# The gate product of the output weights moves from VectorE to GpSimd inside the attention phase

## The chip, the cores and the metric

The kernel runs on one core of a Trainium2 chip. The metric is the device time of one execution in microseconds, given as the median of several runs. The core's engines are TensorE (PE in the rows, its weight loads PEld), VectorE (DVE), ScalarE (ACT), GpSimd (POOL) and SyncE (SP, which issues transfers here). Each engine runs its own list of instructions in order, and waits on semaphores for the others.

## The reference, cut to what matters

One layer of a latent diffusion backbone: 2048 latent tokens and 256 context tokens of width 1024. A combined projection feeds a convolution group and an eight-head attention group; both are joined by one output projection, whose result is multiplied by the gate `g1` (one number per output column) and added to the residual:

```python
        conv_l = conformer_conv(u_l, conv_dw_w[i], conv_dw_b[i], conv_ln_g[i], conv_ln_b[i])
        y_l = merge_groups(conv_l, attn_l, w_o[i], b_o[i])
        x_mid = layer_norm(ALPHA * x + g1 * y_l, ln1_g[i], ln1_b[i])
```

`merge_groups` joins the two groups' outputs and multiplies them by `w_o`. A convolutional feed-forward part of the same layer follows. The kernel multiplies the gate into the columns of `w_o` beforehand, so that it is not applied to `y_l`.

## The kernel before, in words

**Precision.** Matrix products are made from pairs of values: a high part (a rounded copy) and a low part (the value minus its high part). `sub_lo` (L95) is the helper that makes a low part on the engine it is given, so many instructions bear line 95; they are told apart by tile. `mm3` makes the three matmuls of such a pair.

**Attention.** The loop over `u` runs through 128 query tiles of 128 rows: 8 heads (`h`) of 16 tiles (`qt`). Each iteration, in the written order:
- `scores(u)`: TensorE makes five chunks of scores (15 matmuls, L1044) into PSUM buffers `s`, VectorE takes the row maximum of each (L1046), of all (L1047) and scales it (L1048). The `s` buffers are seven; a tile uses five, and one more for turned values.
- `splits(u - 1)`: TensorE turns a part of the tile before (L1063), VectorE splits it into `pp` (L1068, L1069), and SyncE issues a transposing DMA of the rest, `pT<-ph` (L1080).
- `values`: TensorE's product with the values for the tile four earlier (L1094, L1095). Every fourth iteration `combine` does some small work on VectorE and GpSimd (L1115 to L1117).
- `exps(u)`: ScalarE's five exponentials (L1055) out of the `s` buffers, which they free; then a copy of the output (L1101).
- `his(u)`: ScalarE casts 1792 columns to `ph` (L1073), GpSimd makes their low part (L1074, the large subtraction).
- `k_split` when `qt` is 3 to 8: ScalarE casts (L824), GpSimd subtracts (tile `ktl`). `q_split` when `qt % 4 == 1`: ScalarE casts (L843), GpSimd subtracts (tile `ql`).
- `wo_split` when `u % 4 == 2` in iterations 78 to 106: the eight events of this document, numbered 1 to 8. It prepares one 128 x 512 piece of the output weights (four blocks of rows, two halves of columns).

The phase stands under a manual schedule for all engines: each engine gets its instructions in the order in which the code issues them.

**wo_split.** The piece `wst` is loaded on SyncE two iterations earlier (`wo_ld`, L1127), and the gate row `g1b`, repeated over all partitions, once before (L1183). Then: the product `wst * g1b` (L1139, in place), the cast to `woh` on ScalarE (L1140), and the low part `wol` on the engine given, which is GpSimd in the attention loop. In the code of an event the calls stand in this order:

```python
            his(ph, p32)
            ex[u] = ph, p32
            ...
            if WU <= u < WU + 32 and u % 4 == 2:
                wo_split((u - WU) // 8, (u - WU) // 4 % 2, wpa, G)
```

After the loop `wo_split` is called for blocks 4 to 7 as well; these take the other branch (L1137) with a further factor.

Of the kernel before, what the change touches and what calls it, by code (L numbers as in the profile page):

```python
# [15 lines left out]
ALU = mybir.AluOpType  # L16
# [63 lines left out]
def layer(ctx, tc, t, out):  # L80
    nc = tc.nc
    V, S, G, T = nc.vector, nc.scalar, nc.gpsimd, nc.tensor
# [11 lines left out]
    def sub_lo(eng, lo, full, hi):  # L94
        eng.tensor_tensor(lo, full, hi.bitcast(F32), op=ALU.subtract)  # L95
# [86 lines left out]
    def t2k(name):  # L182
        return p1.tile([P, 512], F32, tag="t2k", name=name, bufs=5)
# [71 lines left out]
    for ci, c0 in enumerate((0, D, 512)):  # L255
        ps = ptile("pada")
        for k in range(KB):
            w = t2k("wada")
# [9 lines left out]
            if k % 3 == 2:  # L268
                kd = ci * 2 + k // 3
                if kd < KB:  # L270
                    w = cvp.tile([P, 512], F32, tag="chn", name="wadad", bufs=3)
# [13 lines left out]
    for kd in range(6, KB):  # L285
        w = cvp.tile([P, 512], F32, tag="chn", name="wadad", bufs=3)
# [640 lines left out]
    for kind, g in stages:  # L927
        off, W = span(g)
        ntile = W // P
        if kind == "kv":  # L930
# [20 lines left out]
            for i in range(ntile):  # L951
                pv = ptile("pv")
                sl = slice(i * P, (i + 1) * P)
# [169 lines left out]
    g1b = wpa.tile([P, D], F32, name="g1b")  # L1123
# [6 lines left out]
    def wo_split(k, c, pl, eng):  # L1130
        w = wst.pop((k, c)) if k < 4 else wraw[k][:, c * 512:(c + 1) * 512]
        sl = slice(c * 512, (c + 1) * 512)
        if c == 0:
            woh[k] = pl.tile([P, D], F32R, name=f"woh{k}")
            wol[k] = pl.tile([P, D], F32R, name=f"wol{k}")
        if k >= 4:
            V.scalar_tensor_tensor(w, w, rv_c[:, k - 4:k - 3], g1b[:, sl], op0=ALU.mult, op1=ALU.mult)  # L1137
        else:
            V.tensor_tensor(w, w, g1b[:, sl], op=ALU.mult)  # L1139
        S.copy(woh[k][:, sl], w)  # L1140
        sub_lo(eng, wol[k][:, sl], w, woh[k][:, sl])

# [26 lines left out]
    for u in range(NU + LAG + 1):  # L1169
# [29 lines left out]
        w = u - LAG  # L1199
# [13 lines left out]
        if u < NU:  # L1213
            ph, p32 = exps(*st.pop(u))
            if w >= 0:
                evac(w, po)
            his(ph, p32)
            ex[u] = ph, p32
            if h + 1 < NH and 3 <= qt < 3 + KC:
                k_split(kstn, h + 1, slice(0, P) if h == 0 else k_half(h + 1, False), k_cols(qt - 3))  # L1220
            if qt % 4 == 1 and u + 4 < NU:
                qs_[u // 4 + 1] = q_split(ql_)
            if WU <= u < WU + 32 and u % 4 == 2:
                wo_split((u - WU) // 8, (u - WU) // 4 % 2, wpa, G)
            if u in (NU - 5, NU - 3, NU - 1):
                tt = (u - NU + 5) // 2
                if tt == 0:
                    e_hl = at1.tile([P, 2, 2, 4, P], F32R, tag="oh", name="e_hl", bufs=1)
                if tt < 2:
                    eh, el = e_hl[:, 0, tt], e_hl[:, 1, tt]  # L1230
                else:
                    e2 = k_tile().bitcast(F32R)[:, 0:1024].rearrange("p (s k n) -> p s k n", s=2, k=4)
                    eh, el = e2[:, 0], e2[:, 1]
                conv_split(early[tt], eh, el, G)
                early[tt] = (eh, el)
        elif w < NU:
            evac(w, po)
            wo_split(4 + u - NU, 0, wpb, V)
            wo_split(4 + u - NU, 1, wpb, G)
# [778 lines left out]
```

## Time and profile before

| what | value |
|---|---|
| median of 3 runs | 2864.55 us |
| lowest and highest | 2861.65 and 2869.92 us |
| the profiled execution's own time | 2868.03 us |
| its span, first to last instruction | 2866.3 us |
| TensorE busy | 2715.9 us, 95% |
| VectorE busy | 2257.8 us, 79% |
| ScalarE busy | 1699.1 us, 59% |
| GpSimd busy | 1605.1 us, 56% |
| chain that ended last | TensorE 64%, VectorE 13%, DMA 9%, ScalarE 6%, GpSimd 3% |

The rows further on come from one profiled execution. A row of a timeline gives the start, the duration, the engine, the line, the operation, the tile written and the tiles read, their shapes, how many alike are merged, and in brackets how long the engine stood idle before it and who released it. The shares of the table are means over phases with different bounds, so the phase of the change is read by itself.

### The profile page before, as it was taken

To read this page: it belongs to the slowest core of one execution; us is meant where nothing else is said; L and a number is where in the kernel's file an instruction comes from. 1 tells how busy PE (TensorE), PEld (TensorE's weight loads), DVE (VectorE), ACT (ScalarE), POOL (GpSimd) and SP (SyncE) were. 2 spreads that over 40 slices of the span, in tenths; PEclk is the share of its full clock that TensorE was granted. 3 is DMA by queue.
4 is the path that set the end of the run, shared out by engine and by line. 5 is a ranking of instruction groups with operands and counts; after the bars stand their busy time and mean duration, and the time that the engine had idled before them with its cause. 6 is when DMAs were issued, how large, how long until landed. Compare 5 with 4: busy or idle time off the path is not lost.

```text
span 2866.3 us, 46525 instructions
## 1 busy us (share of the span) xinstructions
PE 2715.9 (95%) x16222; PEld 2246.7 (78%) x16222; DVE 2257.8 (79%) x3918; ACT 1699.1 (59%) x3210; POOL 1605.1 (56%) x1131
## 2 busy tenths in 40 slices
PE   7999899899999999999898999999999999999988
PEld 4888787678888888887776888887778777888766
DVE  5767897888888899878857888887976888554787
ACT  3345456489989989876556555556555555433333
POOL 2235355578888898877435455546444443432555
PEclk8999999999999999999999999999999999999999
DMA  8742227599999999995388755657865788854665
GB/s 287 240 127 66 66 74 229 160 198 206 206 204 202 218 204 212 206 208 185 130 255 268 242 202 184 209 180 247 298 225 174 268 282 282 252 174 143 194 193 178
DMA packets 815483, 578.89 MB, mean 202 GB/s; under 512 B 505616, under 2 KB 654224, under 8 KB 814736
## 3 DMA queue, kind: packets, MB, share of 16 engines
q1 hardware_dynamic: 809136, 558.89, 71.6%
q10 hardware_dynamic: 6112, 17.04, 2.4%
q8 instruction: 127, 2.08, 0.3%
q14 instruction: 108, 0.88, 0.1%
HBM read 294.06 MB, written 164.31 MB: 160 GB/s over the span
## 4 chain that ended last, share of the span: by engine, by line
PE 64%; DVE 13%; DMA 9%; ACT 6%; issue 5%; POOL 3%; SPq 1%; ACTq 0%; DVEq 0%; POOLq 0%
PE px L1436 14%; PE s L1044 11%; PE prod L1436 10%; PE o L1094 4%; PE down L100 3%; PE down L98 3%; PE down L99 3%; DVE mx L1046 2%; PE o L1095 2%; PE tp L1063 1%; PE y L98 1%; PE y L99 1%; PE y L100 1%; DMA d_q<-qo 1%; DMA pT<-ph 1%
## 5 line engine op out<-in xcount | busy, mean ns | idle before, releaser
L1074 POOL TENSOR_TENSOR ph<-p,ph 128x1792 f16<-128x1792 f32 x128 | 463.2, 3619 | 98.2 <-ACT ph L1073 96.2
L1046 DVE TENSOR_REDUCE mx<-s 128x1 f32<-128x512 f32 (+1 forms) x640 | 389.4, 635 | 55.4 <-PE s L1044 52.8
L1055 ACT ACTIVATE p<-s,mx 128x512 f32<-128x512 f32 (+1 forms) x640 | 356.9, 649 | 72.6 <-DVE mx L1048 69.0
L95 POOL TENSOR_TENSOR wul<-s,wuh 128x512 fp32r<-128x512 f32 x176 | 243.9, 1391 | 238.0 <-ACT wuh L1427 224.3
L1436 PE MATMUL px<-oh,wuh 128*128 128x512 f32 x700 | 280.5, 401 | 19.0 <-ACT u L1770 9.9
L95 POOL TENSOR_TENSOR wul<-a,wuh 128x512 fp32r<-128x512 f32 x132 | 180.2, 1370 | 190.3 <-ACT wuh L1427 174.3
L1436 PE MATMUL px<-ol,wuh 128*128 128x512 f32 x700 | 277.5, 397 | 2.7 <-DVE ol L95 2.3
L1436 PE MATMUL px<-oh,wul 128*128 128x512 f32 x700 | 277.4, 396 | 0.0
L1044 PE MATMUL s<-kth,qh 128*128 128x512 f32 (+1 forms) x640 | 250.4, 391 | 13.2 <-ACT p L1055 7.7
L100 PE MATMUL down<-wdh,al 128*128 128x512 f32 x616 | 244.4, 397 | 8.9 <-DVE al L95 6.8
L98 PE MATMUL down<-wdh,ah 128*128 128x512 f32 x616 | 243.7, 396 | 7.4 <-ACT ah L1600 7.4
L99 PE MATMUL down<-wdl,ah 128*128 128x512 f32 x616 | 243.0, 394 | 0.0
L1044 PE MATMUL s<-kth,ql 128*128 128x512 f32 (+1 forms) x640 | 238.5, 373 | 0.2 <-POOL ql L95 0.2
L1044 PE MATMUL s<-ktl,qh 128*128 128x512 f32 (+1 forms) x640 | 237.8, 372 | 0.0
L1073 ACT CAST ph<-p 128x1792 f16<-128x1792 f32 x128 | 218.8, 1710 | 0.1
L1600 ACT CAST ah<-act 128x512 fp32r<-128x512 f32 x168 | 96.1, 583 | 188.6 <-PE down L99 138.1
L1436 PE MATMUL prod<-ol,wuh 128*128 128x512 f32 x524 | 206.4, 394 | 1.3 <-DVE ol L95 0.7
L1436 PE MATMUL prod<-oh,wuh 128*128 128x512 f32 x524 | 206.1, 393 | 0.4 <-ACT oh L1348 0.4
L1436 PE MATMUL prod<-oh,wul 128*128 128x512 f32 x524 | 205.9, 393 | 0.0
L1427 ACT CAST wuh<-s 128x512 fp32r<-128x512 f32 x176 | 108.6, 619 | 142.1 <-DVE s L1415 51.8
L1094 PE MATMUL o<-vh,pT 128*128 128x129 f16 x1792 | 173.0, 220 | 5.4 <-DMA pT<-ph 5.4
L1436 PEld LDWEIGHTS px<-oh,wuh 128*128 128x128 f32 x700 | 132.5, 189 | 57.5 <-ACT u L1770 15.1
(405 smaller groups left out, 7782.5 us busy)
## 6 DMA issues: line engine op xcount, KB each, us to landing
a<-in_w_up SPq DMA_DIRECT2D x154, 256.0 KB, 4.4
d_ws<-s SPq DMA_DIRECT2D x88, 256.0 KB, 2.3
s<-d_ws SPq DMA_DIRECT2D x88, 256.0 KB, 3.9
d_s<-sa SPq DMA_DIRECT2D x88, 256.0 KB, 3.2
d_t<-tw SPq DMA_DIRECT2D x77, 256.0 KB, 3.4
wd<-d_t SPq DMA_DIRECT2D x77, 256.0 KB, 3.9
sa<-d_act SPq DMA_DIRECT2D x66, 256.0 KB, 4.6
wada<-in_w_ada SPq DMA_DIRECT2D x16, 1024.0 KB, 5.7
```

The lines of the kernel that those rows point to most:

```text
L95: eng.tensor_tensor(lo, full, hi.bitcast(F32), op=ALU.subtract)
L98: T.matmul(ps, lhsT=lh, rhs=rh, start=first, stop=False)
L99: T.matmul(ps, lhsT=lh, rhs=rl, start=False, stop=False)
L100: T.matmul(ps, lhsT=ll, rhs=rh, start=False, stop=last)
L1044: T.matmul(ps[:, :w], lhsT=lq[:, qs], rhs=ks[:, c0:c0 + w], start=(n == 0), stop=(n == 2))
L1046: V.tensor_reduce(mx[:, a:a + 1], sl[a], axis=AX.X, op=ALU.max)
L1055: S.activation(p32[:, c0:c0 + w], sl[a], AF.Exp, scale=SCALE, bias=mx[:, NC_ + 1:NC_ + 2])
L1073: S.copy(ph[:, 0, :], p32[:, PT:])
L1074: G.tensor_tensor(ph[:, 1, :], p32[:, PT:], ph[:, 0, :], op=ALU.subtract)
L1094: T.matmul(po[:, 0:129], lhsT=hi, rhs=vh[:, kb, 0:129], start=(kb == 0), stop=False)
L1427: S.copy(h, w)
L1436: T.matmul(ps, lhsT=lw[:, k, :], rhs=rx[:, k, :], start=(fresh and k == 0 and n == 0), stop=(k == 3 and n == 2), skip_group_check=not fresh)
```

## The change

One line of `wo_split` is given to another engine: the product of a piece of the output weights with the gate row, in its branch for `k < 4`, is issued to GpSimd (`G`) in place of VectorE (`V`). The branch for `k >= 4` stays on VectorE.

```diff
@@ -1136,7 +1136,7 @@
         if k >= 4:
             V.scalar_tensor_tensor(w, w, rv_c[:, k - 4:k - 3], g1b[:, sl], op0=ALU.mult, op1=ALU.mult)
         else:
-            V.tensor_tensor(w, w, g1b[:, sl], op=ALU.mult)
+            G.tensor_tensor(w, w, g1b[:, sl], op=ALU.mult)
         S.copy(woh[k][:, sl], w)
         sub_lo(eng, wol[k][:, sl], w, woh[k][:, sl])
```

## Rows read from the trace of the kernel before

**Rows 1.** The head of the profile's page.

```profile
span 2866.3 us, 46525 instructions
```

**Rows 2.** Busy time by stretch: an ordinary part of attention, and the events' stretch.

```profile
core 0: us, PE busy (x) PEld busy (x) DVE busy (x) ACT busy (x) POOL busy (x), PEclk, DMA share, GB/s
700.00:800.00 100.00, 99.80 (x1056) 89.00 (x1054) 89.65 (x180) 93.29 (x149) 88.89 (x43) 1.00 1.12 206
990.00:1170.00 180.00, 170.23 (x1764) 149.00 (x1763) 168.21 (x306) 159.30 (x254) 159.94 (x77) 1.00 1.14 209
```

**Rows 3.** Timeline (start us, us, engine, line, operation), VectorE: tiles 48, 64, 76, 112.

```profile
840.31 0.16 DVE L1047 TENSOR_REDUCE mx<-mx 128x1 f32<-128x5 f32 x1
...
924.11 0.16 DVE L1047 TENSOR_REDUCE mx<-mx 128x1 f32<-128x5 f32 x1
...
988.53 0.16 DVE L1047 TENSOR_REDUCE mx<-mx 128x1 f32<-128x5 f32 x1
...
1188.78 0.16 DVE L1047 TENSOR_REDUCE mx<-mx 128x1 f32<-128x5 f32 x1
```

**Rows 4.** TensorE's waits, 990 to 1170 us: total us, times, longest us.

```profile
PE s L1044 <- ACT p L1055: 5.9, 6, 1.6
...
PE o L1094 <- DMA pT<-ph: 1.3, 2, 0.7
```

**Rows 5.** Instructions that touch tile wst: ns min/median/max, first and last start us.

```profile
L1139 DVE TENSOR_TENSOR wst<-wst,g1b x8: 2392/2414/4146, 1000.5 to 1157.7; 128x512 f32<-128x512 f32 x8
...
L95 POOL TENSOR_TENSOR wol<-wst,woh x8: 1260/1282/1297, 1007.6 to 1165.2; 128x512 fp32r<-128x512 f32 x8
```

**Rows 6.** The same view for lines 1137 and 1503, both after attention.

```profile
L1137 DVE SCALAR_TENSOR_TENSOR wraw<-wraw,rv_c,g1b x8: 726/742/1770, 1270.9 to 1291.2; 128x512 f32<-128x512 f32 x8
...
L1503 POOL TENSOR_TENSOR g1b<-g1b,bo x2: 1287/1508/1729, 1290.7 to 1293.4; 128x512 f32<-128x512 f32 x2
```

**Rows 7.** Timeline of VectorE, event 1.

```profile
1000.54 2.43 DVE L1139 TENSOR_TENSOR wst<-wst,g1b 128x512 f32<-128x512 f32 x1
```

**Rows 8.** Timeline of GpSimd, event 1 and the tile before.

```profile
998.79 3.63 POOL L1074 TENSOR_TENSOR ph<-p,ph 128x1792 f16<-128x1792 f32 x1 [1.59 <-ACT ph L1073]
1002.37 1.74 POOL L95 TENSOR_TENSOR ql<-qst,qh 128x512 fp32r<-128x512 f32 x1
1004.07 3.60 POOL L1074 TENSOR_TENSOR ph<-p,ph 128x1792 f16<-128x1792 f32 x1
1007.62 1.29 POOL L95 TENSOR_TENSOR wol<-wst,woh 128x512 fp32r<-128x512 f32 x1
```

**Rows 9.** Timeline of ScalarE, event 1.

```profile
1002.21 1.71 ACT L1073 CAST ph<-p 128x1792 f16<-128x1792 f32 x1
1003.81 0.64 ACT L1140 CAST woh<-wst 128x512 fp32r<-128x512 f32 x1
1006.17 2.42 ACT L1055 ACTIVATE p<-s,mx 128x512 f32<-128x512 f32 x4 [1.73 <-DVE mx L1048]
```

**Rows 10.** Timeline of TensorE, event 1.

```profile
1006.91 0.50 PE L1044 MATMUL s<-kth,qh 128*128 128x512 f32 x1 [0.72 <-ACT p L1055]
```

**Rows 11.** Timelines of GpSimd and of ScalarE, event 3.

```profile
1052.93 1.01 POOL L95 TENSOR_TENSOR ktl<-kst,kth 64x384 fp32r<-64x384 f32 x1
1053.91 1.26 POOL L95 TENSOR_TENSOR wol<-wst,woh 128x512 fp32r<-128x512 f32 x1
...
1050.49 1.84 ACT L1055 ACTIVATE p<-s,mx 128x512 f32<-128x512 f32 x3 [1.20 <-DVE mx L1048]
```

**Rows 12.** Timelines of GpSimd and of ScalarE, event 4.

```profile
1074.33 1.27 POOL L95 TENSOR_TENSOR wol<-wst,woh 128x512 fp32r<-128x512 f32 x1
...
1074.12 2.79 ACT L1055 ACTIVATE p<-s,mx 128x512 f32<-128x512 f32 x5 [2.55 <-DVE mx L1048]
```

**Rows 13.** Busy time by stretch (columns as in rows 2), before the events.

```profile
799.80:802.16 2.36, 0.00 (x0) 0.00 (x0) 1.56 (x4) 2.33 (x5) 2.20 (x4) 1.00 1.17 249
802.90:806.30 3.40, 3.40 (x22) 2.92 (x19) 0.69 (x1) 2.38 (x4) 3.24 (x3) 0.50 1.18 173
```

## The prediction

> **What bounds the kernel now.** The change touches only a step that runs in the attention phase, so that phase is read first. The page's head gives a span of 2866.3 us [rows 1]; the execution itself took 2868.03 us, 1.7 us more than its span and 3.5 us above the median of 2864.55 us, so the sum below is made against 2868.03 and the same difference is then put on the median. The table of stretches [rows 2] shows TensorE busy 99.80 of 100 us in an ordinary part of attention, at a granted clock of 1.00: TensorE is the bound there, and any time in which it stands still is lost for good. The second row of that table is the stretch in which the eight products of line 1139 run: 170.23 busy of 180, so 9.8 us of standing still.
>
> To see what these eight events cost now, take the starts of the row maximum's last step (one per query tile of 128 rows) [rows 3]. Tiles 48 to 64 are undisturbed: 924.11 - 840.31 = 83.80 us for 16, or 5.237 us a tile. The 36 tiles from 76 to 112 hold all eight events: 1188.78 - 988.53 = 200.25 us, against 36 x 5.237 = 188.5. So the events now cost **11.7 us** together, product, cast, subtraction and all. That is the most that the change could give back. The view of TensorE's waits says on what: 5.9 us on the exponentials (ACT, line 1055) and 1.3 us on a DMA [rows 4], among others.
>
> Why so much for eight small products? One takes 2.4 us at the median and 4.1 us at the longest [rows 5], while the sister product on VectorE, of the same size, takes 0.74 us where GpSimd leaves it alone [rows 6]. The first event shows it: VectorE's product begins at 1000.54 and ends at 1002.97 [rows 7], just after GpSimd's subtraction for the tile before has ended (998.79 + 3.63 = 1002.42) [rows 8]. VectorE stands waiting for GpSimd; the maxima of the next tile stand behind the product and come late, its exponentials are held for 1.73 us (at 1006.17) [rows 9], and TensorE, which needs the score buffers that they free, misses 0.72 us [rows 10].
>
> **What the change removes.** Eight products leave VectorE. Its maxima then come on time, and GpSimd's `ql` subtraction, which ran 1.74 us beside the product [rows 8] against the 1.28 of a `wol` of its size [rows 5], gets 0.46 us back. Taken by itself that is worth up to the 11.7 us above.
>
> **What it adds, and where.** All engines follow the written order in this phase. In the iteration of an event, GpSimd is given: the large `ph` subtraction of this tile (line 1074), perhaps a `ktl` subtraction (k_split), then wo_split. So the product stands behind `ph` on GpSimd's queue, where it stood on VectorE's queue ahead of the next maxima. ScalarE has, straight behind its cast of `ph`, the cast `woh` (line 1140), which reads the product, and behind that the exponentials of the next tile. ScalarE works in order, so the exponentials now wait for `ph`'s subtraction, the product and the cast. Step by step for event 1:
> - GpSimd: `ph` from 1004.07, free for the next at 1007.62, where `wol` starts today [rows 8]. `wol` has the same size and type of input; its median is 1.282 us [rows 5], and I take 1.28 for the product: it ends at 1008.90. No row has this very operation; the bounds are 1.26 (the shortest `wol`) [rows 5] and 1.73 (an addition of that size with g1b, the longer of two) [rows 6].
> - ScalarE: `woh` begins about 0.1 us later at 1009.0 (today 1003.81) and takes 0.64 [rows 9], so the exponentials begin at 1009.6 instead of 1006.17: 3.4 us later.
> - TensorE: it resumes 0.74 us after the exponentials begin (1006.91 against 1006.17) [rows 9, 10], and it is already waiting there. So the shift comes through in full: a wait of 0.7 + 3.4 = 4.1 us.
> Events 2, 5 and 6 have the same pattern (3.4 each). In events 3 and 7 a `ktl` subtraction of 1.0 us stands in front as well: `wol` starts at 1053.91, so the exponentials would begin at 1053.91 + 1.28 + 0.1 + 0.64 = 1055.9, less 0.4 that the `ql` and `ktl` in front no longer lose to VectorE, against 1050.49 today [rows 11]: 5.0; for event 7 the same working gives 5.4. Event 4 is the one whose product took 4.15 us, so it loses least anew: 1074.33 + 2.0 - 0.5 = 1075.9 against 1074.12 [rows 12]: 1.8. Event 8, read in the same way, gets 3.0. Sum: 4 x 3.4 + 5.0 + 5.4 + 1.8 + 3.0 = 28.8 us. From it goes the DMA wait of this stretch, 1.3 us in two pieces [rows 4], of which I let the longer waits cover 1.1: **+27.7 us** of new waits.
> - `wol` and the next `ph` on GpSimd are behind the product too: GpSimd stands 0.8 us for `woh`. The next `ph` waits for ScalarE's cast of it anyway, which now comes 3.4 us later, so that costs nothing more. The 159.94 us that GpSimd is busy of 180 [rows 2] grow by 8 x 1.28 = 10 while the stretch grows by more. The next `wst` load, which waits for `wol`, stands on SyncE's queue two tiles further on in the code, behind a transposing DMA that waits for `ph`, so a `wol` that ends 3.4 us later does not hold it.
>
> The Trainium skill (GPSIMD Engine Reference, 4.1 Engine selection) advises VectorE for elementwise work and puts GpSimd at about twice VectorE's time for two inputs. By that the product would take 2 x 0.74 = 1.48 instead of 1.28 and the sum would be 1.6 us more; the rows of `wol` say 1.28.
>
> **The clock.** Waits of 4.1 us do more than stop TensorE. Earlier in this phase it stood from 799.80 to 802.16, 2.36 us with no matmul; the granted clock then read 0.50 (1.2 of 2.4 GHz) from 802.90 to 806.30 [rows 13]. Through the eight events of today, whose waits are below 1.7 us, it read 1.00 [rows 2]. At half clock, 3.4 us hold 1.7 us of work less. The new waits are nearly twice 2.36 us, so I expect the drop after each; part of the slow stretch may fall into the wait, so I take 1.5 us an event: 8 x 1.5 = **+12 us**, with bounds 0 and 8 x 1.7 = 13.6.
>
> **Sum.** 27.7 + 12 = 39.7: 2868.0 + 39.7 = 2907.7 for an execution like the profiled one, and 2864.55 + 39.7 = **2904 us** beside the median: 1.4% slower.
>
> **Rivals.**
> A. The product is not held behind `ph`: it runs in a gap of GpSimd's queue ahead of it, so that ScalarE finds it ready. Then the events lose VectorE's wait and nothing takes its place: at best 11.7 us go, and the time is 2853 us, 0.4% faster. For it: in the iteration before the event GpSimd is idle for 1.59 us [rows 8]. Against it: the order on GpSimd in the events is that of the code (`ql`, `ph`, `wol`; `ph`, `ktl`, `wol`) [rows 8, 11]. The point that decides is whether `ph` of the same tile comes first. The Trainium skill (SBUF — State Buffer, "SBUF: two separate sides") says that GpSimd and a two-input VectorE instruction exclude each other for a whole instruction; by that alone the change would bring this gain, and the 2.43 us of line 1139 agree with it. 5%.
> B. The waits come, the clock stays up. 27.7 us alone: 2892 us, 1.0% slower. For it: the one 1.7 us wait of today's event 4 passed without a drop; against it the 2.36 us case. 15%.
> C. The wait is shorter than worked out, because buffers of scores let TensorE run ahead or the product is cheap, so that new and old waits cancel: 2864 us, within 0.3%. It would need 28 us to vanish; TensorE already waits at this very place in today's events. 4%.
> D. GpSimd falls behind where k_split loads it, and the backlog of events 3 and 7 spreads, or the product takes 1.73 (8 x 0.45 = 3.6 us): 39.7 + 3.6 + 6 for one more wait like these = 2914 us. 12%.
> The forecast itself, waits with the clock's drop, has 64%.
>
> **How the numbers follow.** A measurement of this kernel can tell about 0.3%, or 8.6 us, from no change. Faster by more than that is rival A, 0.05; the same is C, 0.04; slower is the rest, 0.91. The range reaches from below B (2892, less some 5 us for the two light events) to above D: 2887 to 2918; A and C lie outside.
>
> **What would show it.** Right: no product on VectorE, eight of 1.2 to 1.5 us on GpSimd, each right behind `ph` or `ktl`; `woh` waits on ScalarE for GpSimd, about 5 us a time; TensorE's waits for the exponentials in this stretch rise from 5.9 to some 35 us in about eight waits of 4 to 6 us; stretches of half clock behind them; maxima on VectorE no longer late. Tiles 76 to 112 take some 240 us. Nothing outside the stretch changes. Wrong: if `woh` is ready when its cast of `ph` ends (A), if the clock reads 1.00 throughout (B), or if TensorE does not wait at the exponentials (C).

## The result, and the profile after

The changed kernel takes **2895.25 us** at the median against 2866.79 us of the kernel before in the same comparison: a ratio of 1.0102, 95% interval 1.0084 to 1.0120, so 1.0% or 28.5 us slower. A second comparison gave 1.0110 (1.0087 to 1.0133). The forecast was 2904 us in a range of 2887 to 2918, slower with 0.91.

The product is where the code puts it. The view of the instructions that touch `wst`, the changed kernel (ns min/median/max, first and last start in us; then who waited, us in total and times):

```profile
L1139 POOL TENSOR_TENSOR wst<-wst,g1b x8: 1252/1262/1275, 999.6 to 1186.1; 128x512 f32<-128x512 f32 x8
...
  ACT woh L1140: 42.0, 8
```

Eight products of 1.26 us on GpSimd stand in place of eight of 2.4 us and more on VectorE [rows 5], and ScalarE's cast `woh` waits for every one of them, 42.0 us in all, 5 us a time. The timelines of GpSimd, ScalarE and TensorE in event 1 show the chain, to be held against [rows 8 to 10]:

```profile
993.54 1.31 POOL L95 TENSOR_TENSOR ql<-qst,qh 128x512 fp32r<-128x512 f32 x1
996.01 3.60 POOL L1074 TENSOR_TENSOR ph<-p,ph 128x1792 f16<-128x1792 f32 x1 [1.17 <-ACT ph L1073]
999.57 1.26 POOL L1139 TENSOR_TENSOR wst<-wst,g1b 128x512 f32<-128x512 f32 x1
1001.57 1.28 POOL L95 TENSOR_TENSOR wol<-wst,woh 128x512 fp32r<-128x512 f32 x1 [0.73 <-ACT woh L1140]
...
994.23 1.71 ACT L1073 CAST ph<-p 128x1792 f16<-128x1792 f32 x1
1000.87 0.62 ACT L1140 CAST woh<-wst 128x512 fp32r<-128x512 f32 x1 [4.93 <-POOL wst L1139]
1001.39 1.26 ACT L1055 ACTIVATE p<-s,mx 128x512 f32<-128x512 f32 x2
...
998.53 0.40 PE L1044 MATMUL s<-kth,ql 128*128 128x512 f32 x1
1002.13 0.50 PE L1044 MATMUL s<-kth,qh 128*128 128x512 f32 x1 [3.20 <-ACT p L1055]
```

The product follows `ph`'s subtraction, `woh` waits 4.93 us for it, the exponentials come behind `woh`, and TensorE, resuming 0.74 us after the first of them, has stood for 3.20 us, where it stood for 0.72 [rows 10]. `ql` takes 1.31 us where it took 1.74 [rows 8]: with no product on VectorE, nothing holds it up.

TensorE's waits in the stretch of the events, the changed kernel, and its busy times in that stretch and in four pieces of it (columns as in [rows 2]):

```profile
PE s L1044 <- ACT p L1055: 29.4, 8, 5.6
PE o L1094 <- DMA pT<-ph: 0.7, 1, 0.7
...
979.00:1215.00 236.00, 205.91 (x1997) 179.90 (x1996) 170.22 (x336) 177.45 (x282) 183.96 (x92) 0.92 0.93 178
...
1003.42:1006.84 3.42, 3.42 (x28) 3.26 (x27) 3.05 (x7) 3.42 (x6) 0.84 (x1) 0.50 1.12 206
1027.32:1034.14 6.82, 6.01 (x35) 5.37 (x36) 3.54 (x8) 6.55 (x12) 3.41 (x2) 0.50 0.88 198
1080.15:1083.34 3.19, 0.01 (x2) 0.01 (x1) 0.73 (x2) 1.26 (x3) 2.46 (x3) 1.00 0.78 148
1083.34:1090.00 6.66, 6.66 (x61) 5.80 (x62) 5.20 (x11) 6.66 (x13) 3.50 (x2) 1.00 0.79 178
```

Eight waits, 29.4 us: six of 3.2, one of 4.6, one of 5.6. The granted clock is 0.92 over the stretch, where it was 1.00 [rows 2]. Behind seven of the waits it reads 0.50, for 3.4 us (events 1, 5 and 6) or 6.8 us (events 2, 3, 7 and 8); behind that of event 4 it stays at 1.00. That makes the clock's price readable without any other run. The row maxima (one of them per tile; a stretch of four tiles holds one event):

```profile
979.71 0.16 DVE L1047 TENSOR_REDUCE mx<-mx 128x1 f32<-128x5 f32 x1
...
990.97 0.16 DVE L1047 TENSOR_REDUCE mx<-mx 128x1 f32<-128x5 f32 x1
...
1016.97 0.16 DVE L1047 TENSOR_REDUCE mx<-mx 128x1 f32<-128x5 f32 x1
...
1044.14 0.16 DVE L1047 TENSOR_REDUCE mx<-mx 128x1 f32<-128x5 f32 x1
...
1072.16 0.16 DVE L1047 TENSOR_REDUCE mx<-mx 128x1 f32<-128x5 f32 x1
...
1096.58 0.16 DVE L1047 TENSOR_REDUCE mx<-mx 128x1 f32<-128x5 f32 x1
...
1214.92 0.16 DVE L1047 TENSOR_REDUCE mx<-mx 128x1 f32<-128x5 f32 x1
```

Four undisturbed tiles take 4 x 5.237 = 20.95 us. Event 4 (1072.16 to 1096.58) takes 24.42, 3.5 more: its wait of 3.2 us and 0.3 us beside it, with no half clock. Event 1 (990.97 to 1016.97) takes 26.00 with the same wait: 1.6 us for 3.4 us of half clock. Event 2 (1016.97 to 1044.14) takes 27.17: 2.75 us for 6.8 us. Tiles 76 to 112 (979.71 to 1214.92) take 235.2 us: 46.7 above the undisturbed pace of 188.5, of which 29.4 are the waits and 0.7 a DMA wait. Of the remaining 16.6 us, 8 x 0.29 = 2.3 are what event 4 shows without half clock; some 14 us are what half clock took. Against the 200.25 us of [rows 3] the tiles take 35.0 us more; the stretch behind tile 112 differs by 1.5 us.

Why do the medians differ by 28.5 and these two traces by 35.0 in their tiles? The two profiled executions themselves, 2895.72 and 2868.03 us, differ by only 27.7: that of before came to its first row maximum 7.9 us later (588.0 against 580.1 us) and took 0.9 us more from there to tile 76. Whether these 8 us belong to the change, and whether the 11.7 us of the events before are fixed, the first run below tells.

### The profile page after: what moved, and what is told of

Read it like the earlier page. It is cut to its first block, busy times and chain, and to the rows that moved or that the text cites. A ratio compares the mean times of both kernels' runs of the same rounds, so it can differ in the third digit from the quotient of the medians.

```text
span 2893.9 us, 46506 instructions
## 1 busy us (share of the span) xinstructions
PE 2727.4 (94%) x16222; PEld 2256.4 (78%) x16222; DVE 2243.1 (78%) x3910; ACT 1699.0 (59%) x3210; POOL 1603.8 (55%) x1139
```

## Experiments

**The kernel before, once more.** No edit.

> The kernel before, unchanged, profiled once more. The changed kernel gained 8 us ahead of attention (its first row maximum comes at 580.1 us, that of before at 588.0) which no step of the prediction names. If that is a difference between executions, the first maximum of this trace falls anywhere between about 578 and 590 us; if it belongs to the program of before, it falls at 588 within 1 us. Tiles 76 to 112 should take 200.25 us again, within 1 us.

It came out at a ratio of 1.0011 (0.9995 to 1.0027) to itself, 2865.46 us. The first maximum came at 579.60 us: the 8 us ahead of attention differ between executions and have nothing to do with the change. (Over the runs of this study the first maximum lies between 579 and 589.) The other expectation was missed: tiles 76 to 112 took 205.84 us, 5.6 more than in the first trace, and all of it in the four tiles of event 4 (29.2 us against 23.6). The timelines of VectorE and of GpSimd there, TensorE's wait and the busy times around its end (columns as in [rows 2]) show why:

```profile
1055.89 7.71 DVE L1139 TENSOR_TENSOR wst<-wst,g1b 128x512 f32<-128x512 f32 x1
1063.53 2.80 DVE L1046 TENSOR_REDUCE mx<-s 128x1 f32<-128x512 f32 x5
...
1054.63 3.61 POOL L1074 TENSOR_TENSOR ph<-p,ph 128x1792 f16<-128x1792 f32 x1
1058.20 1.29 POOL L95 TENSOR_TENSOR ql<-qst,qh 128x512 fp32r<-128x512 f32 x1
1059.46 3.59 POOL L1074 TENSOR_TENSOR ph<-p,ph 128x1792 f16<-128x1792 f32 x1
1064.33 1.26 POOL L95 TENSOR_TENSOR wol<-wst,woh 128x512 fp32r<-128x512 f32 x1 [1.28 <-ACT woh L1140]
...
1067.54 0.80 PE L1044 MATMUL s<-kth,qh 128*128 128x512 f32 x1 [4.90 <-ACT p L1055]
...
1065.30:1072.00 6.70, 4.46 (x12) 3.59 (x12) 4.82 (x11) 4.52 (x7) 0.89 (x2) 0.50 1.14 212
```

VectorE's product stood through three GpSimd instructions, 7.71 us, until GpSimd itself had nothing to do; TensorE then missed 4.90 us, and half clock came on top, in the kernel before as well. In the first trace of before the product of the same event took 4.15 us [rows 5], TensorE's longest wait was 1.6 us [rows 4], and the clock stayed at 1.00 [rows 2]. So the price of the kernel before is not fixed: 11.7 us in one trace, 17.3 (205.84 - 188.5) in the other. The gain that the change could at best bring was larger than the prediction's 11.7, and the loss against before is 27 to 35 us in these tiles, by execution (233.1 or 235.2 against 205.84 or 200.25; the 233.1 is from the next run). The 28.5 us of the medians lie in that range.

**The changed kernel, once more.** No edit.

> The changed kernel once more. The product's place in the queue decides the wait, so the eight waits of TensorE should come out alike again: six of 3.2 us, one of 4.6 and one of 5.6. The half-clock stretches behind them may differ in number and length. Tiles 76 to 112 take 235 us within 3 us; the parts ahead of attention may differ by several microseconds.

2894.13 us, ratio 1.0110 (1.0087 to 1.0133). The waits were alike to 0.1 us: 29.3 us in eight, the longest 5.5. Tiles 76 to 112 took 233.1 us; event 2 had 3.4 us of half clock instead of 6.8. The waits belong to the program, the length of the slow stretches to the execution.

**The cast comes one tile later.** The product stays behind `ph` on GpSimd.

```diff
-            if WU <= u < WU + 32 and u % 4 == 2:
-                wo_split((u - WU) // 8, (u - WU) // 4 % 2, wpa, G)
+            if WU <= u < WU + 32 and u % 4 == 2:
+                wo_mul((u - WU) // 8, (u - WU) // 4 % 2)
+            if WU <= u < WU + 32 and u % 4 == 3:
+                wo_split((u - WU) // 8, (u - WU) // 4 % 2, wpa, G)
```

(`wo_mul` is the product alone; `wo_split` is left with the cast and the low part.)

> Product on GpSimd in the same place behind ph; only the cast woh and the low part wol come one tile later. Theory (ScalarE's cast, held by the product behind ph, holds the exponentials): the waits of TensorE go, and with them the half clock; tiles 76 to 112 take 189 to 194 us and the time is 8 to 11 us below before, some 2857. Rival (GpSimd is simply loaded with eight more products and falls behind): GpSimd does the same work, so the time stays near the changed kernel, 2885 to 2895.

2861.4 us, ratio 0.9986 (0.9969 to 1.0004): 34 us below the changed kernel, although GpSimd does the same work and the product stands at the same place. The rival falls: GpSimd's load is not what costs the changed kernel its time. Over before, less than half of the expected 8 to 11 us came, and the interval takes in no change. The profiled execution, one of the two longest of its twelve, shows a new wait. TensorE's waits, and the longest of them on its timeline:

```profile
PE o L1094 <- DMA pT<-ph: 18.4, 5, 8.3
PE s L1044 <- ACT p L1055: 2.0, 2, 1.7
...
1020.42 0.29 PE L1094 MATMUL o<-vh,pT 128*128 128x129 f16 x1 [8.27 <-DMA pT<-ph]
```

The waits for the exponentials have gone from 29.4 to 2.0 us; in their place TensorE waits 18.4 us for the transposing DMAs, 8.3 of it at once, and the clock reads 0.50 for 10.2 us beside each of the two longest waits, so that tiles 76 to 112 still take 215.6 us in this execution.

**The product one tile earlier, ahead of `ph`.**

```diff
+            if WU <= u < WU + 32 and u % 4 == 1:
+                wo_mul((u - WU) // 8, (u - WU) // 4 % 2)
             if qt % 4 == 1 and u + 4 < NU:
                 qs_[u // 4 + 1] = q_split(ql_)
```

> Product on GpSimd one tile earlier, ahead of the event tile's ph, so that it is ready when ScalarE comes to the cast. Theory (place in the queue): no wait of woh, tiles 76 to 112 take 189 to 193 us, time 8 to 11 us below before, some 2857. Rival (GpSimd's load): ph of the event tile starts 1 us later and what waits for it too, time at or above before, 2867 to 2880.

2863.29 us, ratio 0.9996 (0.9982 to 1.0011). Tiles 76 to 112 took 193.1 us, at the end of what the theory expected, in the shortest of twelve executions; of the whole time less than the expected 8 to 11 us showed. It was run again:

> The run that put the product ahead of ph, profiled and timed once more: its median lay 2 us below before although its profiled execution gained 7 us in tiles 76 to 112. If executions differ in the waits for transposing DMAs, this profile shows other waits for pT than the 3.3 us of the first, and tiles 76 to 112 between 190 and 215 us; the ratio to before stays within 0.995 and 1.001.

2858.68 us, ratio 0.9978 (0.9960 to 0.9997); tiles 76 to 112 took 195.0 us. The two traces hardly differ in the waits for transposing DMAs: 3.9 us against 3.3 from 950 to 1250 us, so these do not explain why the medians gained less than the tiles. The timelines of GpSimd and ScalarE in event 1 of this second run, and TensorE's waits:

```profile
993.84 1.30 POOL L1132 TENSOR_TENSOR wst<-wst,g1b 128x512 f32<-128x512 f32 x1
995.09 1.28 POOL L95 TENSOR_TENSOR ql<-qst,qh 128x512 fp32r<-128x512 f32 x1
996.32 3.63 POOL L1074 TENSOR_TENSOR ph<-p,ph 128x1792 f16<-128x1792 f32 x1
...
995.28 0.64 ACT L1142 CAST woh<-wst 128x512 fp32r<-128x512 f32 x1
996.01 2.79 ACT L1055 ACTIVATE p<-s,mx 128x512 f32<-128x512 f32 x5
...
PE o L1094 <- DMA pT<-ph: 2.2, 2, 1.9
PE s L1044 <- POOL ql L95: 2.0, 2, 1.0
```

This is rival A of the prediction, made true: with the product ahead of `ph`, `woh` runs straight behind ScalarE's cast of `ph`, no wait for the exponentials is left (the 2.0 us are waits for `ql`, which now stands behind the product), and the tiles stand 4.5 and 6.5 us above the undisturbed pace instead of 46.7, with the same eight products on the same engine. By the ratios to before it beats the changed kernel by 30 to 38 us. Whether it beats the kernel before is less clear: 0.04% and 0.22% by the two comparisons, the second alone with an interval that leaves out 1.

**The product behind `ql` instead.** The same edit with `wo_mul` below `q_split`.

> Product on GpSimd one tile earlier as in the run that put it ahead of ph, but behind the ql subtraction instead of ahead of it, so that the scores do not wait for ql. ScalarE waits about 1 us for the product at woh, which TensorE's slack of some 0.8 us nearly covers. Tiles 76 to 112 take 189 to 193 us, and the time is 5 to 11 us below before; if GpSimd's load were what costs, it would be no better than before.

A miss: 2867.55 us, ratio 1.0019 (1.0005 to 1.0032). Its profiled execution took 212.4 us in tiles 76 to 112, and the waits for the exponentials were only 3.8 us of it; 14.2 us were waits for transposing DMAs. It was one of the three longest of twelve executions. That the time is no better than before is what the expectation's last sentence says of GpSimd's load; whether the late DMAs hang on that load, no run shows.

**The loads of `wst` earlier as well.** The product ahead of `ph`; the load one tile sooner, into one of two buffers.

```diff
-            if WU <= u < WU + 32 and u % 4 == 0:
-                wo_ld((u - WU) // 8, (u - WU) // 4 % 2, wpa, 1)
+            if WU - 1 <= u < WU + 31 and u % 4 == 3:
+                wo_ld((u + 1 - WU) // 8, (u + 1 - WU) // 4 % 2, at, 2)
```

> As the run that puts the product ahead of ph, and each wst piece is loaded one tile earlier into one of two buffers, so that its load no longer falls into the tile in which the kst and vh loads of ScalarE's queue are issued. Theory (with the product's wait gone, TensorE waits for transposing DMAs that are slowed where the wst load falls together with those loads): the transposing DMAs of 10 to 14 us go, TensorE's waits for pT stay below 4 us, tiles 76 to 112 take 189 to 194 us, and the time is 6 to 11 us below before. Rival (the long transposing DMAs have nothing to do with the wst loads): waits for pT of up to 15 us in some executions, time like before, 2860 to 2868.

2859.0 us, ratio 0.9985 (0.9967 to 1.0003), with 8.6 us of waits for transposing DMAs in the events' stretch and 203.4 us for tiles 76 to 112, in the longest of twelve executions: the theory that the `wst` loads make them late is not borne out. What makes a transposing DMA late stays open. The traces hold one hint: in the three with long waits, the longest transposing DMA of each (14.05, 11.31 and 8.93 us, with a median of 4.9) was issued 3.0 to 3.3 us after a load of `kst` on ScalarE's queue. But in the first run with the product ahead of `ph` the same loads went by with no transposing DMA above 7.5 us, and no run moved them.

**Idle matmuls in the wait**, to tell the waits from the clock.

```diff
             ps = pss.tile([P, 512], F32, tag="s", name="s", bufs=7)
+            if a == 1 and u % 4 == 0 and WU + 4 <= u < WU + 36:
+                for _ in range(FILL):
+                    T.matmul(ps, lhsT=qh[:, qs], rhs=kth[e][:, c0:c0 + w], start=True, stop=True)
```

> The changed kernel, with twelve idle matmuls of 0.23 us (2.8 us) put into TensorE's wait of each event, ahead of its second chunk of scores, whose buffer they overwrite before it is used. TensorE has no more than 0.6 us of standing still left in six events and 2 to 3 us in the other two. Theory (part of the loss is the half clock that follows the waits): the granted clock stays at 1.00 in most events and the time falls by 8 to 14 us against the changed kernel, to 2881 to 2887. Rival (the waits are all of the loss): no change, 2895.

2891.31 us, ratio 1.0093 (1.0071 to 1.0115), on four runs, and not the 2881 to 2887 us expected. The times do not tell it from the changed kernel, but the stretch does. The row of busy times, with TensorE's waits (the edit moves lines by 4):

```profile
979.00:1210.00 231.00, 221.94 (x2141) 192.50 (x2139) 174.44 (x345) 181.21 (x290) 189.18 (x95) 0.99 0.98 186
...
PE s L1048 <- ACT p L1059: 9.1, 9, 3.3
```

The granted clock is 0.99 where it was 0.92; only events 3 and 7, which kept waits of 2.8 and 3.3 us, still have 3.4 us of half clock behind them. Tiles 76 to 112 took 225.5 us, 9.7 less than in the changed kernel, although the exponentials come as late (`woh` waits 43.2 us, against 42.0). By the row maxima 9.0 of it lie in the five events that lost their half clock (1, 2, 5, 6 and 8: 131.8 us became 122.8); event 4, which had none, takes the same 24.4 us, and events 3 and 7 gain nothing. So in these five events 9.0 us of the loss are the clock, as the theory has it; the rest is the wait that the idle matmuls fill.

**Each product twice**, the first result overwritten later.

```diff
+            G.tensor_tensor(wol[k][:, sl], w, g1b[:, sl], op=ALU.mult)
             G.tensor_tensor(w, w, g1b[:, sl], op=ALU.mult)
```

> The changed kernel with each product made twice on GpSimd (the first result goes to a place that is overwritten later). Theory (what stands ahead of the cast woh on GpSimd's queue passes through ScalarE to TensorE in full): each wait grows by the 1.26 us of one product, tiles 76 to 112 by 8 x 1.26 = 10 us to about 245, a little more if the clock falls longer; time some 10 to 13 us above the changed kernel. Rival (TensorE's wait has some other cause, and the product's own time is covered): no change, 235 us.

2908.59 us, ratio 1.0160 (1.0136 to 1.0183). TensorE's waits, and its row in event 1:

```profile
PE s L1044 <- ACT p L1055: 39.8, 8, 6.7
...
1002.29 0.50 PE L1044 MATMUL s<-kth,qh 128*128 128x512 f32 x1 [4.55 <-ACT p L1055]
```

39.8 - 29.4 = 10.4 us more in eight waits, 1.3 each; tiles 76 to 112 took 245.8 us, 10.6 more. The median is 14.5 us above the changed kernel's in the same comparison, a little over the expected 10 to 13. What stands ahead of `woh` on GpSimd reaches TensorE in full.

**A PSUM buffer of its own for the turned tile**: the tag `s` with 6 buffers, `tp` with a tag and one buffer.

```diff
-            ps = pss.tile([P, 512], F32, tag="s", name="s", bufs=7)
+            ps = pss.tile([P, 512], F32, tag="s", name="s", bufs=6)
...
-        tp = pss.tile([P, PT], F32, tag="s", name="tp", bufs=7)
+        tp = pss.tile([P, PT], F32, tag="tp", name="tp", bufs=1)
```

> The changed kernel with the turned tile given a PSUM buffer of its own and the scores six instead of a common seven, so that the second chunk of scores always needs a buffer that the exponentials free. Theory (in the changed kernel TensorE runs one chunk further before it waits, because the second chunk got the buffer of the turned tile): the wait begins after three matmuls instead of six, each of the eight is 0.69 us longer, 3.9 us in six events, and tiles 76 to 112 take 5 to 7 us more, 240 to 242; other tiles keep their 5.2 us. Rival (the buffer plays no part): 235 us and waits of 3.2 us.

2903.78 us, ratio 1.0143 (1.0119 to 1.0166). TensorE's row in event 1:

```profile
1011.36 0.67 PE L1044 MATMUL s<-kth,qh 128*128 128x512 f32 x1 [3.92 <-ACT p L1055]
```

The wait comes after three matmuls and is 3.92 us, 0.72 more than in the changed kernel: the buffer decides where TensorE stops. Six of the eight waits grew by 0.7 us so, that of event 7 by 0.3, and in event 2 TensorE had spent most of it on a transposing DMA just before. Tiles 76 to 112 took 238.1 us, 2.9 more where 5 to 7 were expected; half clock came to 37.5 us in both traces. The medians differ by 9.7 us; the tiles account for 2.9 of these, and the profiled execution also came to its first maximum 8.3 us later than that of the changed kernel (588.4 against 580.1).

## Why the prediction was right, and where its sizes were off

- **The place in the queue** was right, and it is shown: delaying the cast takes the wait away, moving the product ahead of `ph` takes it away, doubling the product lengthens it by a product. Rival A's point of decision, whether `ph` of the tile comes first, decided.
- **The price of the product** was right: 1.26 against 1.28. The Trainium skill's factor of two (GPSIMD Engine Reference, 4.1 Engine selection) would have been 1.48 by the prediction's estimate; against the sister product's 0.74 us [rows 6] the trace gives 1.26 / 0.74 = 1.7.
- **The new waits were too large**: 28.8 us forecast, less 1.1 for a DMA wait. TensorE's waits for exponentials and turned tiles rose from 8.4 us (5.9 [rows 4] and the 2.5 that the same view gives for the turned tile) to 29.4, so 21.0; the DMA waits fell by 0.6. The step that failed is "it is already waiting there. So the shift comes through in full: a wait of 0.7 + 3.4 = 4.1 us". It was 3.2. In the kernel before, the second chunk of scores in this event needs a buffer that the exponentials free; in the changed kernel it has the buffer of the turned tile. The two programs' instruction lists say so for the fourth matmul of that tile: it waits for ScalarE before the change, and for VectorE and TensorE after it. The timelines agree: TensorE stops before that matmul at 1006.91 [rows 10], and in the changed kernel three matmuls later, at 1002.13.

  So TensorE gets one chunk of three matmuls (0.7 us) further before it stops, and a buffer of its own for the turned tile undoes that (3.92 us). The remaining 0.2 us is in ScalarE's chain: the exponentials start 5.45 us after the end of the cast of `ph` (1001.39 - 995.94), worked out as 1009.6 - 1003.92 = 5.7. Why the pool hands out its buffers in another order once the product has left VectorE was not tried.

  "Events 2, 5 and 6 have the same pattern (3.4 each)" failed as well. In events 2 and 6 the second chunk had the turned tile's buffer before the change too, and TensorE waited 1.27 us there for VectorE, which empties it; so these waits grew by 1.9 us only, those of events 1 and 5 by 2.5. (Two slips without weight: event 4's working gives 1074.33 + 2.0 - 0.5 = 1075.83, so 1.7 and not 1.8, and its wait before was 1.6 us and not 1.7 [rows 4].) The rows of the kernel before, TensorE's waits and event 2:

```profile
PE s L1044 <- DVE pp L1069: 2.5, 2, 1.3
...
1029.40 0.48 PE L1044 MATMUL s<-kth,qh 128*128 128x512 f32 x1 [1.27 <-DVE pp L1069]
```

- **The clock was a little too small**: 12 us forecast, some 14 found. The mechanism held in seven of eight events; the step that was mis-sized is "At half clock, 3.4 us hold 1.7 us of work less", since four of the seven stretches were 6.8 us long, and that of event 2 cost 2.75. Rival B falls.
- Together: 21.0 + 16.6 less the 2.6 us by which the events cost more than TensorE's waits before (1.3 of DMA waits, of which 0.7 stay, and the 2.0 that are left of the 11.7) gives the 35.0 us found between the two traces; forecast 39.7. That the sum lies nearer than the waits alone is luck: one term was too large and the other too small.
- **The base was taken as fixed**: "the events now cost 11.7 us". The second trace of before has 17.3. And the execution that the sum was made against was 8 us late ahead of attention, as the second trace (579.6 us) and those of the changed kernel were not. Of the 11.2 us between the forecast's 39.7 and the medians' 28.5, the terms above explain 4.7; the other 6.5 are such differences between executions, whose shares no run separates.
- GpSimd did not fall behind (rival D): TensorE has eight waits, one an event, and none more behind events 3 and 7. The new waits did not cancel with the old ones (rival C).

## What to carry to other kernels

Moving an instruction to another engine moves it into that engine's queue: before its own duration, look at what stands ahead of it there and at which in-order engine has to wait for its result. Here 1.26 us behind a subtraction of 3.6 us cost some 30 us, and the same instruction one tile earlier brought the time back to that of before, or a little below. And when a wait at the bounding engine is gone, look for the next: in three of the five traces of the variants without it, waits for transposing DMAs took its place (8.6 to 18.4 us). Before a sum is made against one trace, take a second one of the same kernel: here its tiles 76 to 112 differed by 5.6 us and the start of attention by 8.4 us.

## What the runs showed of the hardware

- A VectorE product with two SBUF inputs took 2.4, 4.15 and 7.71 us in the same program beside GpSimd's back-to-back subtractions, against 0.74 us of a like product where GpSimd leaves it alone. The Trainium skill (SBUF — State Buffer, "SBUF: two separate sides") says that whichever of the two starts first keeps the shared ports for its whole instruction and the other blocks. The traces agree: the product ended 0.55 us after GpSimd did, in the 2.43 us case [rows 7, 8] as in the 7.71 us one. But in the 7.71 us case it stood through three GpSimd instructions (1054.63 to 1063.05), until GpSimd was idle.
- Equal waits of TensorE of 3.2 us were followed by no half clock (event 4), by 3.4 us of it (event 1) and by 6.8 us (event 2), which cost 0, 1.6 and 2.75 us on top. A wait of 2.36 us was followed by 3.4 us of it in the kernel before [rows 13]. Filling the waits with idle matmuls kept the clock at 1.00 in the five events where they filled all but 0.5 us and it had fallen without them.
- Two programs that differ in one instruction's engine hand out their PSUM buffers in another order here, and that moved the point at which TensorE stops by one chunk, 0.7 us.
